# Feed-forward weights in units of four blocks: one load tile, one split and kept slots in a two-layer hybrid trunk

## The chip, the cores and the metric

The kernel runs on one core of one Trainium2 chip. The metric is device time in microseconds (us). TensorE (PE in the profile) does the matrix products, VectorE (DVE) and ScalarE (ACT) work on tiles in on-chip memory, GpSimd (POOL) does a few small things, and SyncE (SP) issues nearly all of the data transfers (DMA). Each engine takes its instructions strictly in the order in which they were put into its queue, and waits at an instruction until what it needs is there.

## The reference

The reference is a decoder trunk of two pre-norm residual layers on an input of 256 rows (positions) by 2048 columns, all in float32:

```python
def reference(...):
    h = x
    for layer in range(DEPTH):            # DEPTH = 2
        xn = rms_norm(h, norm_mix[layer])
        if layer % 2 == 0:
            mix = swa_mlstm_mixer(xn, w_in_even[j], w_out_even[j], ...)
        else:
            mix = forgetting_attention_mixer(xn, w_in_odd[j], fox_b_f[j], w_out_odd[j])
        h = h + mix
        h = h + swiglu(rms_norm(h, norm_ffn[layer]), w_gate[layer], w_up[layer], w_down[layer])
    return rms_norm(h, norm_final)

def swiglu(xn, w_gate, w_up, w_down):
    return (jax.nn.silu(xn @ w_gate) * (xn @ w_up)) @ w_down
```

The first layer's mixer is a sliding-window attention (16 heads) beside an mLSTM (4 heads), the second's is an attention with forget gates (16 heads). Each mixer has a wide input projection and an output projection of 2048 by 2048. The feed-forward part (FFN) has a hidden size of 5632, so three matrices of 2048 by 5632, and makes up most of the work.

## The kernel before

**Products.** A float32 product is made of three matmuls in a faster format. A matrix is split into `hi`, the value rounded to that format, and `lo`, the rest; the function `three` (line 508) adds hi·xh, lo·xh and hi·xl into one accumulator. The activations (`xh`, `xl`, `mh`, `ml`) are split once. The weights stream from memory: a block of 128 rows by 512 columns at a time is loaded raw, ScalarE copies it to `hi` (line 177 or 339), VectorE subtracts to get `lo` (line 178 or 340), and TensorE uses both. A plain load covers two blocks (`CK = 2`).

**Plain and mixed pairs.** `pair_group` (line 516) computes two column stripes of 512 at once, for the FFN a stripe of gate and one of up, or two stripes of down. It walks over pairs of row blocks in the order given by `ORDER` or `DOWN`. A plain pair takes eight `three` (24 matmuls). A mixed pair uses a scheme of the Strassen kind with seven (21 matmuls): it needs sums and differences of the weight blocks (`ta`, `tb`, `tc_`, `td`, lines 568 to 571, on VectorE), which are split as well, into the tiles `ht` and `lt`. It also needs sums of the activations (`sx`, `sd`), which are formed ahead. The mixed pairs collect four products `prods` in accumulators of their own over the whole group; at the group's end `combine` (line 523) works them into a tile `c` that is added to the plain accumulators.

**Stages.** A layer's FFN has 11 gate/up groups, in three parts (3, 4 and 4 groups). Each has 8 positions: 5 plain and 3 mixed pairs. After each gate/up group, `ffn` (line 599) adds (line 619), applies silu on ScalarE (line 621) and multiplies (line 623); then the result is turned, by DMA transposes on SP (line 648) or, for the last group of the first part, on TensorE. The turned values are joined and split into `mh`, `ml` some positions later. Each part ends with two down groups. `close_layer` (line 712) opens the pool `fp` for one layer's output projection (`out_proj`, line 493, through `gemm`) and its FFN.

**Buffers.** Before, pool `wp` gives six tiles each of `hi` and `lo`, two blocks a tile; pool `wr` four raw tiles of two blocks. In the FFN, the mixed pairs have four raw tiles of their own in `fp`, two tiles each of `ht` and `lt`, and a tile `t4` for two of the sums.

**Order.** The kernel is written as one loop nest; a planner at build time moves instructions among the engines' queues by its own costs and by which buffers are free, and what it gives is fixed: TensorE's queue mixes matmuls of several positions, and heads of the mixers with matmuls of a projection. How many buffers there are and when they come free therefore changes the order on every engine.

Of the kernel before, what the change touches and what calls it, by code (L numbers as in the profile page):

```python
# [17 lines left out]
P = 128  # L18
# [6 lines left out]
CK = 2  # L25
# [25 lines left out]
LATER_DOWN = (5, 6)  # L51
RAWS = 4
P_JOIN = 4
# [19 lines left out]
def trunk(  # L73
# [42 lines left out]

    def load_raw(w, k0, c0, n, pool=wr, bufs=4, raws=None):
        if raws:
            raw = raws.pop(0)
            raws.append(raw)  # L120
        else:
            raw = pool.tile([P, CK, NB], F32, tag="raw", name="raw", bufs=bufs)
        loaded[0] = nc.sync.dma_start(
            raw[:, :, 0:n], w[k0 * P : (k0 + CK) * P, c0 : c0 + n].rearrange("(k p) n -> p k n", p=P)
        )
        return raw
# [12 lines left out]
    load_x(0, CK)  # L139
    first = wr.tile([P, CK, NB], F32, tag="raw", name="raw", bufs=4)  # L140
    for k in range(CK):
# [31 lines left out]
    def split_chunk(raw, n):  # L173
        hi = wp.tile([P, CK, NB], F32R, tag="hi", name="hi")
        lo = wp.tile([P, CK, NB], F32R, tag="lo", name="lo")
        for k in (slice(0, 1), slice(1, CK)) if any(raw is f for f in fine) else (slice(0, CK),):
            latest[0] = nc.scalar.copy(hi[:, k, 0:n], raw[:, k, 0:n])  # L177
            nc.vector.tensor_tensor(  # L178
                out=lo[:, k, 0:n], in0=raw[:, k, 0:n], in1=hi[:, k, 0:n].bitcast(F32), op=ALU.subtract
            )  # L180
        return hi, lo

    def new_acc():
# [69 lines left out]
    def sums_of(pool, sh, sl, copies, full=None, tags=("tmp", "tmp"), bufs=None, box=None):  # L253
# [9 lines left out]
        nc.vector.tensor_tensor(out=s[:, 1, :], in0=s[:, 0, :], in1=full[:, 0, 0, :], op=ALU.subtract)  # L263
        nc.vector.tensor_tensor(out=s[:, 2, :], in0=full[:, 0, 0, :], in1=full[:, 0, 1, :], op=ALU.subtract)
        nc.vector.tensor_tensor(out=s[:, 3, :], in0=full[:, 1, 0, :], in1=s[:, 1, :], op=ALU.subtract)
# [61 lines left out]
    def scrap(fp, n):  # L327
        if n % 2 == 0:
            box = fp.tile([P, 4, NB], F32, tag="c", name="box", bufs=1)
            halves = box[:, 0:2, :], box[:, 2:4, :]  # L330
        elif n == 3:
            halves = [fp.tile([P, 3, NB], F32, tag=f"sd{i}", name="box", bufs=1)[:, 0:CK, :] for i in range(2)]
        else:
            halves = [fp.tile([P, CK, NB], F32, tag="raw", name="box", bufs=RAWS) for _ in range(2)]
        flat, turned = (a.rearrange("p a n -> p (a n)") for a in halves)
        return flat, turned.bitcast(U16).rearrange("p (b k t q) -> p b k t q", b=2, t=NT, q=P)
# [179 lines left out]
    def pair_group(fp, par, lhs, sums, mats, order, todo=(), halves=None, inner=None, raws=None):  # L516
# [6 lines left out]
        def combine(prods):  # L523
            c = fp.tile([P, 4, NB], F32, tag="c", name="c", bufs=1)
            nc.scalar.copy(c[:, 0, :], prods[0])
            nc.vector.tensor_tensor(out=c[:, 2, :], in0=prods[3], in1=c[:, 0, :], op=ALU.add)
            nc.vector.tensor_tensor(out=c[:, 1, :], in0=prods[2], in1=c[:, 2, :], op=ALU.add)
# [4 lines left out]
        for pos, (kind, pair) in enumerate(order):  # L532
            k0 = 2 * pair
            if inner is not None and pos == len(order) - 1:
                c = combine(prods)
                inner()
            if not kind:
                last = pos == len(order) - 1
                walk = [(i, t) for i in range(CK) for t in range(NT)]
                if last:  # L540
                    walk.sort(key=lambda it: it[1])
                for m, (w, c0) in enumerate(mats):
                    hi, lo = load_chunk(w, k0, c0, NB)
                    run_due(todo, pos)
                    for i, t in walk:
                        ah, al = lhs(k0 + i)
                        ts = slice(t * P, (t + 1) * P)
                        three(
                            plain[m][t], ah[:, ts], al[:, ts], hi[:, i, :], lo[:, i, :],
                            pos == 0 and i == 0, last and i == CK - 1,  # L550
# [3 lines left out]
            if first:  # L554
                prods = [bank(1 - par, "prod") for _ in range(4)]
            ra, rb = (load_raw(w, k0, c0, NB, fp, W_RAWS if halves else RAWS, raws) for w, c0 in mats)
            hg, lg = split_chunk(ra, NB)
            run_due(todo, pos)
            t4 = ra if halves else fp.tile([P, 2, NB], F32, tag="t4", name="t4", bufs=1)
            ta, tb, tc_, td = (  # L560
                (ra[:, 0, :], rb[:, 0, :], rb[:, 1, :], ra[:, 1, :])
                if halves
                else (t4[:, 0, :], t4[:, 1, :], ra[:, 0, :], ra[:, 1, :])
            )
            hu = wp.tile([P, CK, NB], F32R, tag="hi", name="hi")
            lu = wp.tile([P, CK, NB], F32R, tag="lo", name="lo")
            split_plain(hu[:, 1, :], lu[:, 1, :], rb[:, 1, :])
            nc.vector.tensor_tensor(out=ta, in0=rb[:, 0, :], in1=ra[:, 0, :], op=ALU.subtract)
            nc.vector.tensor_tensor(out=tb, in0=rb[:, 1, :], in1=rb[:, 0, :], op=ALU.subtract)
            nc.vector.tensor_tensor(out=tc_, in0=rb[:, 1, :], in1=ta, op=ALU.subtract)  # L570
            nc.vector.tensor_tensor(out=td, in0=ra[:, 1, :], in1=tc_, op=ALU.subtract)
            parts = []
            for src in (ra, rb) if halves else (t4, ra):
                if halves:
                    hs, ls = halves.pop(0)
                    halves.append((hs, ls))
                else:
                    hs = fp.tile([P, 2, NB], F32R, tag="ht", name="ht")
                    ls = fp.tile([P, 2, NB], F32R, tag="lt", name="lt")
                split_plain(hs, ls, src)  # L580
                parts.append((hs, ls))
            where = ((0, 0), (1, 0), (1, 1), (0, 1)) if halves else ((0, 0), (0, 1), (1, 0), (1, 1))
            ht = [parts[a][0][:, b, :] for a, b in where]
            lt = [parts[a][1][:, b, :] for a, b in where]
            sh, sl = sums(pair)
            xa, la = lhs(k0)
            xb, lb = lhs(k0 + 1)
            three(prods[0], xa[:, t0], la[:, t0], hg[:, 0, :], lg[:, 0, :], first, last)
            three(plain[0][0], xb[:, t0], lb[:, t0], hg[:, 1, :], lg[:, 1, :], False, False)
            three(plain[1][0], sh[:, 3, :], sl[:, 3, :], hu[:, 1, :], lu[:, 1, :], False, False)  # L590
            three(prods[1], sh[:, 0, :], sl[:, 0, :], ht[0], lt[0], first, last)
            three(prods[2], sh[:, 2, :], sl[:, 2, :], ht[1], lt[1], first, last)
            three(prods[3], sh[:, 1, :], sl[:, 1, :], ht[2], lt[2], first, last)
            three(plain[0][1], xb[:, t1], lb[:, t1], ht[3], lt[3], False, False)
        if inner is None:
# [3 lines left out]
    def ffn(layer, fp, sx, sd, key, todo, idx_next=None, key_next=None, finish=None):  # L599
# [6 lines left out]
        for g0, g1 in zip(PARTS, PARTS[1:]):  # L606
# [3 lines left out]
            for g in range(g0, g1):  # L610
# [5 lines left out]
                for m in range(2):  # L616
                    for t in range(NT):
                        o = c[:, 2 * m + t, :]
                        nc.vector.tensor_tensor(out=o, in0=plain[m][t], in1=o, op=ALU.add)
                for t in range(NT):  # L620
                    nc.scalar.activation(c[:, t, :], c[:, t, :], AF.Silu, scale=r[:, t : t + 1])
                for t in range(NT):
                    nc.vector.scalar_tensor_tensor(
                        out=c[:, t, :], in0=c[:, 2 + t, :], scalar=r[:, t : t + 1], in1=c[:, t, :], op0=ALU.mult, op1=ALU.mult
                    )
# [65 lines left out]
            for n0 in (0, 2):  # L691
# [13 lines left out]
                for m in range(2):  # L705
                    for t in range(NT):
                        o = h[:, t, (n0 + m) * NB : (n0 + m + 1) * NB]
                        nc.vector.tensor_tensor(out=o, in0=c[:, 2 * m + t, :], in1=o, op=ALU.add)
# [12 lines left out]

    acc0 = new_acc()
    hi = wp.tile([P, CK, NB], F32R, tag="hi", name="hi")
    lo = wp.tile([P, CK, NB], F32R, tag="lo", name="lo")
    latest[0] = latest_warm
# [596 lines left out]
```

## Time and profile before

| | |
|---|---|
| median of 3 runs | 2077.82 us |
| lowest and highest | 2076.74 and 2078.33 us |
| span of the profiled execution | 2076.6 us |
| granted TensorE clock, mean | 0.999 |
| TensorE busy | 2066.4 us |
| VectorE busy | 1824.5 us, 2410 instructions |
| ScalarE busy | 1374.7 us, 1736 instructions |
| DMA | 434.87 MB, 209 GB/s on the mean |

The times are those of whole executions. The profile is of one execution; its span, from its first to its last instruction, is 2076.6 us, and no separate time of that execution is given, so the span stands for it; the median of the runs is 1.2 us more. In a line of groups of instructions one reads the line of the kernel, the engine, the operation, output and inputs by the program's names with the tile's shape, the count, the busy time in us and the mean length in ns, then how long the engine had been idle before these and what ended it. In a line of the timeline the two first numbers are the start and the length in us; the length of an instruction reaches a little into the next, so the distance from start to start is what the engine's time is made of.

### The profile page before, as it was taken

Reading aid. Unit: us, or ns where it says so; the run is one execution under the profiler, and the core shown is the slowest. Engines: PE = TensorE matmul, PEld = TensorE weight load, DVE = VectorE, ACT = ScalarE, POOL = GpSimd, SP = SyncE. Lnnn points to the kernel's source line nnn. Section 1 sums busy time; section 2 is a strip of 40 time slices with the busy share of each in tenths; the row PEclk is TensorE's granted clock in tenths of the full one; section 3 lists DMA queues with packets and bytes.
Section 4 is the critical chain, followed back from the end, with each engine's and each line's share of the span. In section 5 each row is a group of like instructions: output and inputs, shape, how many; then the busy total and the mean of one; then the engine's idle time right before and its main releaser. Section 6 shows DMA issues by size and latency. Waiting matters only on the chain.

```text
span 2076.6 us, 26994 instructions
## 1 busy us (share of the span) xinstructions
PE 2066.4 (100%) x9473; PEld 1715.0 (83%) x9473; DVE 1824.5 (88%) x2410; ACT 1374.7 (66%) x1736; POOL 41.7 (2%) x66
## 2 busy tenths in 40 slices
PE   9999999999999999999999999999999999999998
PEld 7878888888888888888888888888888888888887
DVE  6788769999999999999899778689999999999994
ACT  6777678765676656667676776687655667456763
POOL 1010000000000000000000001000000000000000
PEclk9999999999999999999999999999999999999999
DMA  8566577666566666666576866586665667666764
GB/s 292 172 213 188 190 247 236 203 217 206 189 230 223 205 210 205 220 212 204 185 215 204 235 193 184 156 283 220 206 205 200 213 206 234 203 202 213 220 197 138
DMA packets 309575, 434.87 MB, mean 209 GB/s; under 512 B 106412, under 2 KB 114624, under 8 KB 309312
## 3 DMA queue, kind: packets, MB, share of 16 engines
q1 hardware_dynamic: 307088, 426.27, 65.1%
q0 software_dynamic: 1632, 5.80, 0.8%
q8 instruction: 74, 1.21, 0.2%
q10 hardware_dynamic: 720, 1.09, 0.2%
q14 instruction: 61, 0.50, 0.1%
HBM read 408.68 MB, written 2.12 MB: 198 GB/s over the span
## 4 chain that ended last, share of the span: by engine, by line
PE 97%; DVE 1%; ACT 1%; DMA 1%; issue 1%; SPq 0%; POOLq 0%; POOL 0%; ACTq 0%; DVEq 0%
PE acc L510 21%; PE acc L509 21%; PE acc L511 21%; PE acc L213 5%; PE acc L212 5%; PE acc L214 5%; PE prod L509 5%; PE prod L510 5%; PE prod L511 5%; PE p L369 1%; PE po L470 1%; DMA raw<-in_w_in_odd_dram 0%; ACT s L403 0%; PE po L471 0%; DVE lo L178 0%
## 5 line engine op out<-in xcount | busy, mean ns | idle before, releaser
L177 ACT CAST hi<-raw 128x1024 fp32r<-128x1024 f32 (+3 forms) x656 | 664.8, 1028 | 440.2 <-PE acc L511 269.1
L178 DVE TENSOR_TENSOR lo<-raw,hi 128x1024 fp32r<-128x1024 f32 (+3 forms) x656 | 772.8, 1192 | 146.3 <-ACT hi L177 143.5
L510 PE MATMUL acc<-lo,xh 128*128 128x512 f32 x1254 | 488.6, 390 | 0.0
L509 PE MATMUL acc<-hi,xh 128*128 128x512 f32 x1254 | 485.9, 390 | 0.5 <-ACT hi L177 0.5
L511 PE MATMUL acc<-hi,xl 128*128 128x512 f32 x1254 | 484.8, 389 | 0.0
L510 PEld LDWEIGHTS acc<-lo,xh 128*128 128x128 f32 x1254 | 235.4, 188 | 49.4 <-DVE lo L178 0.6
L509 PEld LDWEIGHTS acc<-hi,xh 128*128 128x128 f32 x1254 | 235.2, 188 | 49.5 <-ACT hi L177 0.7
L511 PEld LDWEIGHTS acc<-hi,xl 128*128 128x128 f32 x1254 | 235.4, 188 | 48.8
L510 PE MATMUL acc<-lo,mh 128*128 128x512 f32 x437 | 169.7, 389 | 0.0
L511 PE MATMUL acc<-hi,ml 128*128 128x512 f32 x437 | 168.4, 389 | 0.0
L509 PE MATMUL acc<-hi,mh 128*128 128x512 f32 x437 | 167.9, 389 | 0.0
L339 ACT CAST hi<-raw 128x512 fp32r<-128x512 f32 x109 | 67.6, 620 | 89.4 <-PE acc L511 80.5
L213 PE MATMUL acc<-lo,mh 128*128 128x512 f32 (+1 forms) x322 | 126.3, 392 | 0.0
L212 PE MATMUL acc<-hi,mh 128*128 128x512 f32 (+1 forms) x322 | 125.8, 391 | 0.0
L214 PE MATMUL acc<-hi,ml 128*128 128x512 f32 (+1 forms) x322 | 123.7, 391 | 0.0
L340 DVE TENSOR_TENSOR lt<-t,ht 128x1024 fp32r<-128x1024 f32 x95 | 115.8, 1219 | 5.2 <-ACT ht L339 5.1
L339 ACT CAST ht<-t 128x1024 fp32r<-128x1024 f32 x95 | 99.9, 1051 | 30.7 <-PE prod L511 28.8
L339 ACT CAST ht<-raw 128x1024 fp32r<-128x1024 f32 x95 | 99.7, 1050 | 29.7 <-PE acc L511 15.0
L340 DVE TENSOR_TENSOR lt<-raw,ht 128x1024 fp32r<-128x1024 f32 x95 | 115.7, 1218 | 1.8 <-ACT ht L339 1.8
L213 PE MATMUL acc<-lo,xh 128*128 128x512 f32 (+3 forms) x288 | 99.8, 348 | 0.2 <-DVE lo L178 0.2
L214 PE MATMUL acc<-hi,xl 128*128 128x512 f32 (+3 forms) x288 | 98.1, 344 | 0.0
L212 PE MATMUL acc<-hi,xh 128*128 128x512 f32 (+3 forms) x288 | 95.9, 347 | 0.3
(363 smaller groups left out, 3448.0 us busy)
## 6 DMA issues: line engine op xcount, KB each, us to landing
raw<-in_w_gate_dram SPq DMA_DIRECT2D x176, 512.0 KB, 4.5
raw<-in_w_up_dram SPq DMA_DIRECT2D x176, 512.0 KB, 4.6
raw<-in_w_down_dram SPq DMA_DIRECT2D x176, 512.0 KB, 5.1
raw<-in_w_in_odd_dram SPq DMA_DIRECT2D x88, 512.0 KB, 4.9
raw<-in_w_in_even_dram SPq DMA_DIRECT2D x51, 512.0 KB, 5.0
raw<-in_w_out_even_dram SPq DMA_DIRECT2D x32, 512.0 KB, 5.1
raw<-in_w_out_odd_dram SPq DMA_DIRECT2D x32, 512.0 KB, 4.8
hr<-in_w_in_even_dram SPq DMA_DIRECT2D x12, 512.0 KB, 4.6
```

Of the source, the lines that this page charges most:

```text
L177: latest[0] = nc.scalar.copy(hi[:, k, 0:n], raw[:, k, 0:n])
L178: nc.vector.tensor_tensor(out=lo[:, k, 0:n], in0=raw[:, k, 0:n], in1=hi[:, k, 0:n].bitcast(F32), op=ALU.subtract)
L212: nc.tensor.matmul(o, ah[:, ts], hi, start=(k == 0), stop=False)
L213: nc.tensor.matmul(o, ah[:, ts], lo, start=False, stop=False)
L214: nc.tensor.matmul(o, al[:, ts], hi, start=False, stop=(k == k_all - 1 and cs.stop == n))
L339: nc.scalar.copy(dst_h, src)
L340: nc.vector.tensor_tensor(out=dst_l, in0=src, in1=dst_h.bitcast(F32), op=ALU.subtract)
L369: nc.tensor.matmul(pq[j % 2][:, j // 2, :], q_of(j, b), k_of(j)[:, 0:cols], start=True, stop=True)
L470: nc.tensor.matmul(po, v_of(j, 0), tt[:, j, 0:2, :].rearrange("p c q -> p (c q)"), start=True, stop=False)
L509: nc.tensor.matmul(o, ah, hi, start=start, stop=False)
L510: nc.tensor.matmul(o, ah, lo, start=False, stop=False)
L511: nc.tensor.matmul(o, al, hi, start=False, stop=stop)
```

## The change

The change replaces the weight buffers by rings of slots of four blocks, and makes the FFN use a slot as a whole.

- `weights` is a list of three pairs `hi`, `lo` of four blocks; `raws_` a list of two raw tiles of four blocks. `slot` takes the next one round the ring, `half_slot` half of one, for all code that goes on with two blocks (the projections).
- For a layer's output projection and FFN, `close_layer` takes a fourth pair `hi3`, `lo3` from the pool `fp`, appends it to the ring, and removes it at the end.
- A plain pair in the FFN loads gate and up into one raw tile (two transfers), makes `hi` by two copies of two blocks and `lo` by one subtraction of four blocks.
- A mixed pair in the FFN loads into one raw tile of four blocks in `fp` (`RAWS`, now two of them) by three transfers: two blocks, then one, then one. One copy and one subtraction take the three blocks that are used as they are. The four sums are formed in place, two of them by one instruction whose first operand is repeated. Then two copies and one subtraction of four blocks split them into a second slot of the ring; `ht`, `lt` and `t4` are gone.
- `combine` in the FFN does the last two of its four additions in one instruction. The blocks of `c` stand in another order, two sums have the other sign, and in all mixed pairs the last four `three` stand in another order.

```diff
-RAWS = 4
+RAWS = 2
...
-    wp = ctx.enter_context(tc.tile_pool(name="wp", bufs=6))
-    wr = ctx.enter_context(tc.tile_pool(name="wr", bufs=4))
+    wp = ctx.enter_context(tc.tile_pool(name="wp", bufs=1))
+    weights = [[wp.tile([P, 4, NB], F32R, name=f"{a}{i}") for a in ("hi", "lo")] for i in range(3)]
+    wr = ctx.enter_context(tc.tile_pool(name="wr", bufs=1))
+    raws_ = [[wr.tile([P, 4, NB], F32, name=f"raw{i}")] for i in range(2)]
+    spare = {}
+
+    def slot(ring):
+        spare.pop(id(ring), None)
+        ring.append(ring.pop(0))
+        return ring[-1]
+
+    def half_slot(ring):
+        kept = spare.pop(id(ring), None)
+        if kept:
+            return [t_[:, CK:, :] for t_ in kept]
+        kept = slot(ring)
+        spare[id(ring)] = kept
+        return [t_[:, 0:CK, :] for t_ in kept]
...
     def split_chunk(raw, n):
-        hi = wp.tile([P, CK, NB], F32R, tag="hi", name="hi")
-        lo = wp.tile([P, CK, NB], F32R, tag="lo", name="lo")
+        hi, lo = half_slot(weights)
...
+    def load_rows(dst, w, k0, c0):
+        n = dst.shape[1]
+        loaded[0] = nc.sync.dma_start(
+            dst, w[k0 * P : (k0 + n) * P, c0 : c0 + NB].rearrange("(k p) n -> p k n", p=P)
+        )
+
+    def split_wide(hi, lo, src, parts):
+        for ks in parts:
+            latest[0] = nc.scalar.copy(hi[:, ks, :], src[:, ks, :])
+        nc.vector.tensor_tensor(out=lo, in0=src, in1=hi.bitcast(F32), op=ALU.subtract)
...
             nc.scalar.copy(c[:, 0, :], prods[0])
+            if halves is None:
+                nc.vector.tensor_tensor(out=c[:, 1, :], in0=prods[3], in1=c[:, 0, :], op=ALU.add)
+                nc.vector.tensor_tensor(out=c[:, 2, :], in0=prods[2], in1=c[:, 1, :], op=ALU.add)
+                nc.vector.tensor_tensor(
+                    out=c[:, 1:4:2, :],
+                    in0=prods[1].rearrange("p (a n) -> p a n", a=1).broadcast_to([P, 2, NB]),
+                    in1=c[:, 1:3, :],
+                    op=ALU.add,
+                )
+                return c
...
+                if halves is None:
+                    (raw,) = slot(raws_)
+                    for m, (w, c0) in enumerate(mats):
+                        load_rows(raw[:, CK * m : CK * (m + 1), :], w, k0, c0)
+                    hi, lo = slot(weights)
+                    split_wide(hi, lo, raw, (slice(0, CK), slice(CK, 4)))
+                    run_due(todo, pos)
...
+            if halves is None:
+                raw = fp.tile([P, 4, NB], F32, tag="raw", name="raw", bufs=RAWS)
+                (wa, ca), (wb, cb) = mats
+                load_rows(raw[:, 0:CK, :], wa, k0, ca)
+                for k in range(CK):
+                    load_rows(raw[:, 3 - k : 4 - k, :], wb, k0 + k, cb)
+                hi, lo = slot(weights)
+                split_wide(hi[:, 0:3, :], lo[:, 0:3, :], raw[:, 0:3, :], (slice(0, 3),))
+                run_due(todo, pos)
+                nc.vector.tensor_tensor(
+                    out=raw[:, 0:4:3, :],
+                    in0=raw[:, 3:4, :].broadcast_to([P, 2, NB]),
+                    in1=raw[:, 0:3:2, :],
+                    op=ALU.subtract,
+                )
+                nc.vector.tensor_tensor(out=raw[:, 2, :], in0=raw[:, 2, :], in1=raw[:, 0, :], op=ALU.subtract)
+                nc.vector.tensor_tensor(out=raw[:, 1, :], in0=raw[:, 1, :], in1=raw[:, 2, :], op=ALU.subtract)
+                ht_, lt_ = slot(weights)
+                split_wide(ht_, lt_, raw, (slice(0, CK), slice(CK, 4)))
...
     def close_layer(layer, w_out, idx, key, **rest):
         with tc.tile_pool(name=f"fp{layer}", bufs=2) as fp:
+            fourth = [fp.tile([P, 4, NB], F32R, name=f"{a}3", bufs=1) for a in ("hi", "lo")]
+            weights.append(fourth)
+            spare.clear()
             nx = len(mixed_of(ORDER))
...
             ffn(layer, fp, sx, sd, key, todo, **rest)
+            weights.remove(fourth)
+            spare.clear()
```

More of the change, by code (lines that the diff above doesn't have):

```diff
@@ L120, in load_raw @@
             raws.append(raw)
+        elif pool is None:
+            (raw,) = half_slot(raws_)
         else:
-            raw = pool.tile([P, CK, NB], F32, tag="raw", name="raw", bufs=bufs)
+            raw = pool.tile([P, CK, NB], F32, tag="raw", name="raw", bufs=W_RAWS)
         loaded[0] = nc.sync.dma_start(
@@ L139, in trunk @@
     load_x(0, CK)
-    first = wr.tile([P, CK, NB], F32, tag="raw", name="raw", bufs=4)
+    (first,) = half_slot(raws_)
     for k in range(CK):
@@ L333, in scrap @@
         else:
-            halves = [fp.tile([P, CK, NB], F32, tag="raw", name="box", bufs=RAWS) for _ in range(2)]
+            box = fp.tile([P, 4, NB], F32, tag="raw", name="box", bufs=RAWS)
+            halves = box[:, 0:CK, :], box[:, CK:, :]
         flat, turned = (a.rearrange("p a n -> p (a n)") for a in halves)
@@ L536, in pair_group @@
                 inner()
+            last = pos == len(order) - 1
             if not kind:
-                last = pos == len(order) - 1
                 walk = [(i, t) for i in range(CK) for t in range(NT)]
@@ L555, in pair_group @@
                 prods = [bank(1 - par, "prod") for _ in range(4)]
[L556 to L564, printed above, removed]
@@ L575, in pair_group @@
                     hs, ls = halves.pop(0)
                     halves.append((hs, ls))
[L577 to L583, printed above, removed]
@@ L584, in pair_group @@
-            lt = [parts[a][1][:, b, :] for a, b in where]
+                    split_plain(hs, ls, src)
+                    parts.append((hs, ls))
+                where = ((0, 0), (1, 0), (1, 1), (0, 1))
+                ht = [parts[a][0][:, b, :] for a, b in where]
+                lt = [parts[a][1][:, b, :] for a, b in where]
+                hg = [hg[:, 0, :], hg[:, 1, :], hu[:, 1, :]]
+                lg = [lg[:, 0, :], lg[:, 1, :], lu[:, 1, :]]
             sh, sl = sums(pair)
@@ L707, in ffn @@
                         o = h[:, t, (n0 + m) * NB : (n0 + m + 1) * NB]
-                        nc.vector.tensor_tensor(out=o, in0=c[:, 2 * m + t, :], in1=o, op=ALU.add)
+                        nc.vector.tensor_tensor(out=o, in0=c[:, 2 * t + m, :], in1=o, op=ALU.add)
                 for m in range(2):
```

63 lines of the change are left out of this document (38 added, 25 removed).

## The prediction

> **What bounds the kernel now.** I read the first part of the page, the throttle's row, the chain and TensorE's waits, in this order.
>
> ```profile
> span 2076.6 us, 26994 instructions
> PE 2066.4 (100%) x9473; PEld 1715.0 (83%) x9473; DVE 1824.5 (88%) x2410; ACT 1374.7 (66%) x1736; POOL 41.7 (2%) x66
> PEclk9999999999999999999999999999999999999999
> PE 97%; DVE 1%; ACT 1%; DMA 1%; issue 1%; SPq 0%; POOLq 0%; POOL 0%; ACTq 0%; DVEq 0%
> ```
> ```profile
> PE cold L159 <- POOL ones L156: 1.2, 1, 1.2
> PE acc L509 <- ACT hi L177: 0.5, 1, 0.5
> PE acc L213 <- DVE lo L178: 0.2, 1, 0.2
> ```
>
> TensorE is busy all the time at the full clock, makes 97% of the chain, and waited 1.9 us in all. So an instruction saved on another engine is worth nothing by itself, and the first matmul that has to wait costs its whole wait. The distance between matmuls follows from two rows with 20 matmuls between them: 21 steps in 4.76 us, 0.2267 us each.
>
> ```profile
> 1313.42 0.39 PE L212 MATMUL acc<-hi,mh 128*128 128x512 f32 x1
> ...
> 1318.18 0.39 PE L212 MATMUL acc<-hi,mh 128*128 128x512 f32 x1
> ```
>
> The engine to watch is VectorE. By stretch, in the feed-forward part (columns: stretch, length, then the busy time of PE, PEld, DVE, ACT, POOL, then clock and DMA):
>
> ```profile
> 576.00:617.00 41.00, 41.00 (x183) 33.94 (x182) 39.24 (x51) 28.04 (x31) 0.00 (x0) 1.00 0.63 205
> 596.30:613.80 17.50, 17.50 (x79) 14.48 (x78) 16.65 (x20) 11.89 (x13) 0.00 (x0) 1.00 0.60 172
> ```
>
> A gate/up group takes 5 plain positions of 24 matmuls and 3 mixed of 21, 183 x 0.2267 = 41.5 us. VectorE is busy 96% of the first stretch and TensorE waits for nothing: the buffers let VectorE be late here and early there. Whatever takes that freedom away decides this case.
>
> **The change, part by part.**
>
> *Fewer, longer instructions.* The built program has 1934 VectorE instructions against 2413, 1536 ScalarE against 1631, 95 more weight loads, and the same 9302 matmuls. Prices (columns: start, length):
>
> ```profile
> 663.78 4.62 DVE L178 TENSOR_TENSOR lo<-raw,hi 128x1024 fp32r<-128x1024 f32 x4
> 668.32 1.22 DVE L340 TENSOR_TENSOR lt<-t,ht 128x1024 fp32r<-128x1024 f32 x1
> 669.45 0.68 DVE L526 TENSOR_TENSOR c<-prod,c 128x512 f32<-128x512 f32 x1
> 670.17 0.69 DVE L527 TENSOR_TENSOR c<-prod,c 128x512 f32<-128x512 f32 x1
> ...
> 672.19 0.68 DVE L528 TENSOR_TENSOR c<-prod,c 128x512 f32<-128x512 f32 x1
> 672.79 0.68 DVE L529 TENSOR_TENSOR c<-prod,c 128x512 f32<-128x512 f32 x1
> ```
>
> Start to start, 1024 elements take (668.32 - 663.78)/4 = 1.13 us and 512 take 672.79 - 672.19 = 0.60; one that reads the result of the one just before it 670.17 - 669.45 = 0.72, so 0.12 more. On the line through these, 0.07 + 0.53 per 512, 1536 elements take 1.67 and 2048 take 2.20 us (my estimates; nothing of before is so long). The saving, 479 x 0.07 = 33 us, lies beside TensorE: nothing on the path.
>
> *The boundary between groups, the first loss.* The rows above show it in before: the shifted sums of the next group's first mixed pair (lt, 668.32) are split ahead of the combine (L526, 669.45), in buffers of their own. After the change these sums need a whole slot of four blocks in a ring of four, and that slot is held until the last products of the old group. In the built order, 77 matmuls = 17.48 us lie between the end of a group's last product and the first use of the next pair's split sums. VectorE has to do in them, in this order: combine 0.60 + 0.60, add 0.60, combine of two blocks 1.13, split 1536 for 1.67, three adds 1.80, sums 1.13, split 2048 for 2.20, two scalings 1.32, sum 0.60, split 1536 of the second mixed pair 1.67, sum 0.60, its sums 1.13 + 0.60 + 0.60, and last the split of 2048 that is waited for, 2.20. The scalings go by
>
> ```profile
> 559.08 1.41 DVE L623 SCALAR_TENSOR_TENSOR c<-c,r 128x512 f32<-128x512 f32 x2
> 560.40 0.69 DVE L340 TENSOR_TENSOR lo<-raw,hi 128x512 fp32r<-128x512 f32 x1
> ```
>
> (560.40 - 559.08)/2 = 0.66. The sum is 18.45; three direct dependences 0.36 and the ends (an instruction ends 0.09 after the next may start; start-up behind TensorE) some 0.1 more: 18.9, so 1.4 us late. Counted so for every boundary, 26 of them come out late, by 0.56 to 2.56, together 34 us. Nothing hides it: the list starts at a point of TensorE's own work, so a stall moves the next one along. Ends: without dependences and ends 0.9 x 26 = 23; with the two-block instructions, whose repeated operand no row shows, at the price of two single ones, and the slower dependent price for more of them, 1.8 x 26 = 47. I take 34, the value that the rows give.
>
> *The third mixed pair behind it.* With two raw tiles of four blocks, the third pair's three loads wait for the first pair's last split, and stand on SP's queue behind four transposes:
>
> ```profile
> 603.84 5.87 SPq L648 DMA_TRANSPOSE turned<-c  x4
> 609.82 0.53 SPq L123 DMA_DIRECT2D raw<-in_w_gate_dram  x1
> ```
> ```profile
> raw<-in_w_gate_dram SPq DMA_DIRECT2D x176, 512.0 KB, 4.5
> raw<-in_w_down_dram SPq DMA_DIRECT2D x176, 512.0 KB, 5.1
> ```
> ```profile
> L339 ACT CAST hi<-raw 128x512 fp32r<-128x512 f32 x109 | 67.6, 620 | 89.4 <-PE acc L511 80.5 <-ACT ht L339 4.3 <-issue 2.9
> L177 ACT CAST hi<-raw 128x1024 fp32r<-128x1024 f32 x620 | 643.0, 1051 | 423.5 <-PE acc L511 259.0 <-issue 48.5 <-PE acc L214 45.0
> ```
>
> From the group's last product: 13.3 us of the list above up to the second scaling, one copy 1.05, transposes 5.1 to 5.9 (another boundary's four took 5.1), landing 4.5 to 5.1, the copy of 1536 at 620 + 2 x 431 = 1.48: 25.5 to 27. Its first matmul stands 107 matmuls = 24.3 behind the same point, with the first stall 25.7: late by 0 to 1.3. Sixteen groups are followed so by another gate/up group: 5 to 22 us, and I take 0.8 x 16 = 13. In before the same loads follow the transposes at once, but onto four raw tiles, and no matmul waited.
>
> *The ends of the two mixers.* The fourth slot lies in the feed-forward pool, whose memory the mixers' pools still hold. Work of the output projection that filled TensorE while the last heads were finished now stands behind them. For the last heads of the second layer, before:
>
> ```profile
> 1301.68 1.91 PE L369 MATMUL p<-ktf,qtf 128*128 128x128 f32 x10
> ...
> 1318.41 0.27 PE L456 MATMUL pp<-ident,s 128*128 128x128 f32 x1
> ```
> ```profile
> 1304.57 1.28 DVE L372 SCALAR_TENSOR_TENSOR s<-p,cb 128x512 f32<-128x512 f32 x2
> 1305.88 1.22 DVE L388 TENSOR_REDUCE mx<-s 128x4 f32<-128x1024 f32 x1
> 1313.70 1.93 DVE L416 TENSOR_SCALAR s<-s,rec 128x128 f32<-128x128 f32 x8
> ```
> ```profile
> 1309.81 0.40 ACT L403 ACTIVATE s<-s,neg 128x128 f32<-128x128 f32 x1
> ...
> 1313.24 0.19 ACT L403 ACTIVATION_READ_ACCUMULATOR s<-s,neg 128x1 f32 x1
> ```
>
> Between scores and transposes TensorE had some 15 us of projection. In the new order it has three matmuls, 0.7, and the transposes themselves, 2.4. The softmax needs 0.7 + 1.2 + a split 1.1 + small ones 0.6 (half of it the gap from the last exponential to the scaling) + exponentials 3.6 (1309.81 to 1313.43) + scaling 1.9 = 9.1 to 9.4: stalled 6.3. Ends 5 (without the split) and 9 (the transposes not overlapped). For the mLSTM heads:
>
> ```profile
> 237.23 0.60 PE L1037 MATMUL pom<-ce,qst 128*128 128x257 f32 x2
> 237.67 0.59 PE L1035 MATMUL pom<-ve,dt__1241 128*128 128x257 f32 x2
> ```
> ```profile
> 253.36 0.91 ACT L344 ACTIVATE mh<-room,gT 128x256 fp32r<-128x256 f32 x2
> ```
>
> From a head's last product (L1037, done 237.7) to the first half of its split result, 253.8, lie 16 us, of which nearly 4 are other work that stood between on the two engines. In the new order 11 products at 237.67 - 237.23 = 0.44 and 5 matmuls, 5.9 us, are left there: stalled 6 to 10, I take 8. The upper end is 12, if the second head, which follows closer, adds its own.
>
> *A clock that cools* may add to this. No stretch of before shows it: the clock is 1.00 throughout. The Trainium skill, TensorE: Matmul & The Clock Gate, Part 1, says that an idle window of about 3.4 us halves the clock and that it takes as long to come back; by it, each of the two long stalls would cost 2 to 3.5 us more, an estimate, and the sum 5 us more. The boundary stalls are shorter than its window. I leave it out of the sum.
>
> *Nothing else:* the new order of threes and the signs change no count; 95 loads split in two cost SP 95 x some 0.4 (609.82 to the next issue, 0.5 at most), between issues that wait anyway; if that cover goes, it is in the 13 above.
>
> **Sum.** 34 + 13 + 6.3 + 8 = 61. On the profiled span 2076.6 that is 2138; the median of the runs lies 1.2 above that span: 2139. Ends: 23 + 5 + 5 + 6 = 39 gives 2117; 47 + 22 + 9 + 12 = 90 gives 2168.
>
> **Rivals.**
> *Faster.* VectorE gets through each boundary in time. For: 33 us less of fixed cost. Against: the list is a sum of measured rates, and it is the per-element part that fills the window. It decides from 1.4 us less per boundary, so from 1.5 instead of 2.20 us for a 2048 split. The waits to be won are 1.9 us and the few matmuls that start late, and the mixers' ends must be hidden too: 2072. The Trainium skill, VectorE: DVE Perf Modes, section on the TRN2 errata, says that a large tile pays the fixed cost once and many small ones each time; by that advice alone this would be the case. It speaks of one engine's time, not of when a slot comes free.
> *No change.* The stalls are there only in my count, since leads taken earlier cover them: 2078. Against it: the boundary's list starts at a matmul, no earlier lead enters.
> *Only the mixers' ends stall.* The boundaries are covered, 6.3 + 8: 2092.
> *More.* The late loads push later loads, so each boundary loses 3 us or more where I have 2, and the clock cools: 2077.8 + 26 x 3 + 14 + 5 = 2175.
>
> **How the numbers follow.** 0.2% (4.2 us) is what a measurement tells from no change. My sum within its ends 0.65, only the mixers 0.10, more 0.14, no change 0.05, faster 0.06. Leaving out the upper case's tail and the two lowest cases, the range is 2092 to 2170. Slower 0.89, same 0.05, faster 0.06.
>
> **What would show it.** Waits of the boundary matmuls (TensorE's products prod and acc in the function of the three matmuls) for the long split, L210, some 1 to 2.6 us each; waits of matmuls for a copy, L209, behind late loads; two gaps of 6 to 10 us, ahead of the transposes of the second layer's last heads and of the first layer's projection rows 8 to 11. A split of 2048 that takes 2.3 us confirms the price. If those waits are missing and VectorE idles ahead of the combine, the step on the boundary is wrong.

## The result, and the profile after

The changed kernel takes 2196.23 us (median of 4 runs, 2192.77 to 2201.11) against 2078.07 us before on the same chips: a ratio of 1.0572, 95% interval 1.0555 to 1.0588. The prediction had the direction, slower, and put the size at 61 us; it is 118 us, and 2196 lies above the range. The profiled execution's span grew by 114.5 us.

The first lines of the page of the changed kernel, and its chain:

```profile
span 2191.1 us, 26291 instructions
PE 2103.9 (96%) x9473; PEld 1715.9 (78%) x9473; DVE 1798.8 (82%) x1931; ACT 1353.5 (62%) x1641; POOL 40.7 (2%) x66
PE 38%; DVE 22%; DMA 8%; issue 8%; ACT 7%; SPq 2%; DVEq 0%; ACTq 0%; POOLq 0%; POOL 0%
```

VectorE executes 479 instructions fewer, and is busy 25.7 us less, as the edit says. TensorE is no longer the whole chain: VectorE has 22% of it. TensorE's waits (engine and tile, line, what it waited for: total, times, longest):

```profile
PE prod L540 <- DVE lo L210: 24.8, 22, 1.2
PE prod L539 <- ACT hi L209: 21.0, 31, 2.0
PE pp L486 <- DVE s L446: 7.2, 1, 7.2
PE acc L241 <- ACT mh L374: 7.2, 1, 7.2
PE acc L540 <- DVE lo L210: 5.2, 5, 1.6
PE acc L539 <- DVE h L383: 3.0, 6, 1.1
PE prod L539 <- ACT c L555: 2.7, 2, 1.7
```

Before, all waits were 1.9 us. By TensorE's own landmarks (the first and last matmul of each feed-forward part, from the timelines) the time went to four places:

| stretch | before | after | more |
|---|---|---|---|
| end of the mLSTM and first output projection | 95.4 | 108.0 | 12.6 |
| first feed-forward part and second layer's input projection | 959.4 | 1006.4 | 47.0 |
| last attention heads and second output projection | 98.5 | 111.2 | 12.8 |
| second feed-forward part, up to its last pair group | 644.0 | 686.7 | 42.7 |

The remaining stretches differ by half a microsecond together. One boundary between two gate/up groups, VectorE's timeline of the changed kernel (start, length, idle time ahead in brackets):

```profile
618.10 0.69 DVE L557 TENSOR_TENSOR c<-prod,c 128x512 f32<-128x512 f32 x1 [1.03 <-PE prod L541]
618.89 0.69 DVE L558 TENSOR_TENSOR c<-prod,c 128x512 f32<-128x512 f32 x1
619.50 0.68 DVE L684 TENSOR_TENSOR c<-acc,c 128x512 f32<-128x512 f32 x1
620.10 1.22 DVE L559 TENSOR_TENSOR c<-prod,c 128x1024 f32<-128x1024 f32 x1
621.23 1.75 DVE L210 TENSOR_TENSOR lo<-raw,hi 128x1536 fp32r<-128x1536 f32 x1
622.90 1.88 DVE L684 TENSOR_TENSOR c<-acc,c 128x512 f32<-128x512 f32 x3
624.69 2.28 DVE L210 TENSOR_TENSOR lo<-raw,hi 128x2048 fp32r<-128x2048 f32 x1
626.89 1.22 DVE L615 TENSOR_TENSOR raw<-raw 128x1024 f32<-128x1024 f32 x1
...
631.63 1.22 DVE L615 TENSOR_TENSOR raw<-raw 128x1024 f32<-128x1024 f32 x1
632.76 0.68 DVE L622 TENSOR_TENSOR raw<-raw 128x512 f32<-128x512 f32 x1
633.36 0.68 DVE L621 TENSOR_TENSOR raw<-raw 128x512 f32<-128x512 f32 x1
634.08 0.69 DVE L622 TENSOR_TENSOR raw<-raw 128x512 f32<-128x512 f32 x1
635.00 4.49 DVE L210 TENSOR_TENSOR lo<-raw,hi 128x2048 fp32r<-128x2048 f32 x2 [0.23 <-ACT hi L209]
```

These are the instructions of the prediction's list at its prices; a few neighbours have changed places (the split at 624.69 stands ahead of the sums at 626.89, for one). The list starts when the product that the combine reads first is done, and runs 19.2 us (618.10 to the end of the first of the last two splits, 635.00 + 2.29) with 0.23 us of idle time in it. TensorE's side of the same boundary:

```profile
634.15 0.39 PE L541 MATMUL acc<-hi,sx 128*128 128x512 f32 x1
635.02 0.50 PE L539 MATMUL prod<-hi,sx 128*128 128x512 f32 x1 [0.49 <-ACT hi L209]
635.36 0.39 PE L539 MATMUL acc<-hi,xh 128*128 128x512 f32 x1
635.59 0.63 PE L539 MATMUL prod<-hi,sx 128*128 128x512 f32 x2
637.35 0.55 PE L540 MATMUL prod<-lo,sx 128*128 128x512 f32 x1 [1.13 <-DVE lo L210]
637.70 0.63 PE L541 MATMUL prod<-hi,sx 128*128 128x512 f32 x1
638.13 0.63 PE L540 MATMUL acc<-lo,xh 128*128 128x512 f32 x1
```

There are two waits. The first is for a copy to hi, the second for the split. Each shows in the steps between starts: 0.87 for 0.23 at the first, 1.53 for 0.23 (from the last of the two at 635.59) at the second, so 1.95 us together. The copy follows the first pair's last sum (L622 at 632.76), but not at once. ScalarE's timeline:

```profile
631.08 1.05 ACT L209 CAST hi<-raw 128x1024 fp32r<-128x1024 f32 x1 [3.13 <-DVE raw L621]
632.03 1.99 ACT L716 COPY c<-c 128x1024 uint16<-128x1024 uint16 x2
633.93 2.94 ACT L209 CAST hi<-raw 128x1024 fp32r<-128x1024 f32 x3
```

The sum was done at 633.44. The copy started 0.49 us later, behind the two copies (L716) that prepare the old group's result for the transposes. All 16 first waits of this kind in the trace stand so: the copy follows L716 without idle time, 0.49 us after the end of its sum. VectorE's 0.23 us of idle time ahead of the split is a wait for the same copy.

After each of TensorE's waits, the next step takes 0.34 or 0.35. From 637.70 on, the steps are 0.43: the clock has fallen to half, as the windows of the two stretches of 3.4 us show (columns as before: busy times, then clock and DMA):

```profile
637.70:641.10 3.40, 3.40 (x9) 2.65 (x8) 1.80 (x1) 1.22 (x2) 0.00 (x0) 0.50 0.94 72
641.10:644.50 3.40, 3.40 (x16) 2.80 (x15) 2.29 (x1) 0.90 (x2) 0.00 (x0) 1.00 1.05 373
```

The sum over all feed-forward matmuls of the step less 0.227 us, sorted by what released each, gives for both layers: waits for the long split (L210) 34.9 us; waits for a copy (L209) directly ahead of these 13.0; other waits for copies 16.6; the slow first steps after waits 11.7 (3.0 or less of that before); steps at half clock 6.0; others, such as the residual L383 and the combine's own copy L555, some 9.

The two long gaps:

```profile
253.10 0.80 PE L241 MATMUL acc<-hi,mh 128*128 128x512 f32 x1 [7.17 <-ACT mh L374]
```
```profile
1373.59 1.45 PE L486 MATMUL pp<-ident,s 128*128 128x128 f32 x4 [7.22 <-DVE s L446]
```

After the first the clock stays at one half from 253.10 to 258.8, another 2.8 us lost; after the second until 1378.4, 2.4 us.

### The profile page after: what moved, and what is told of

Its sections match the earlier page's. It is cut to its first block, busy times and chain, and to the rows that moved or that the text cites. A ratio compares the mean times of both kernels' runs of the same rounds, so it can differ in the third digit from the quotient of the medians.

```text
span 2191.1 us, 26291 instructions
## 1 busy us (share of the span) xinstructions
PE 2103.9 (96%) x9473; PEld 1715.9 (78%) x9473; DVE 1798.8 (82%) x1931; ACT 1353.5 (62%) x1641; POOL 40.7 (2%) x66
## 4 chain that ended last, share of the span: by engine, by line
PE 38%; DVE 22%; DMA 8%; issue 8%; ACT 7%; SPq 2%; DVEq 0%; ACTq 0%; POOLq 0%; POOL 0%
PE acc L540 9%; PE acc L541 9%; DVE lo L210 8%; PE acc L539 8%; ACT hi L209 4%; DMA raw<-in_w_up_dram 3%; DMA raw<-in_w_down_dram 3%; DVE raw L615 3%; PE prod L540 2%; PE prod L541 2%; PE prod L539 2%; DVE raw L621 2%; DVE c L684 2%; PE acc L241 1%; PE acc L243 1%
## 5 line engine op out<-in xcount | busy, mean ns | idle before, releaser
L209 ACT CAST hi<-raw 128x1024 fp32r<-128x1024 f32 (+1 forms) x607 | 653.2, 1116 | 506.7 <-PE acc L541 169.6
L210 DVE TENSOR_TENSOR lo<-raw,hi 128x2048 fp32r<-128x2048 f32 (+1 forms) x351 | 745.9, 2143 | 140.2 <-ACT hi L209 139.0
L540 PE MATMUL acc<-lo,xh 128*128 128x512 f32 x1320 | 515.7, 391 | 0.0
L541 PE MATMUL acc<-hi,xl 128*128 128x512 f32 x1320 | 514.3, 390 | 0.0
L196 DVE TENSOR_TENSOR lo<-raw,hi 128x1024 fp32r<-128x1024 f32 (+3 forms) x239 | 270.0, 1145 | 120.7 <-ACT hi L195 119.9
L195 ACT CAST hi<-raw 128x1024 fp32r<-128x1024 f32 (+3 forms) x239 | 230.9, 985 | 140.9 <-PE acc L243 25.8
L615 DVE TENSOR_TENSOR raw<-raw 128x1024 f32<-128x1024 f32 x95 | 116.0, 1221 | 1.0
L540 PEld LDWEIGHTS acc<-lo,mh 128*128 128x128 f32 x466 | 87.8, 189 | 25.4 <-DVE lo L210 7.3
L539 PEld LDWEIGHTS acc<-hi,mh 128*128 128x128 f32 x466 | 87.4, 188 | 21.0 <-ACT mh L369 2.6
L541 PEld LDWEIGHTS acc<-hi,ml 128*128 128x128 f32 x466 | 87.7, 188 | 19.2 <-DVE ml L370 0.7
```

The costliest lines, as they stand in the source:

```text
L196: nc.vector.tensor_tensor(out=lo[:, k, 0:n], in0=raw[:, k, 0:n], in1=hi[:, k, 0:n].bitcast(F32), op=ALU.subtract)
L209: latest[0] = nc.scalar.copy(hi[:, ks, :], src[:, ks, :])
L210: nc.vector.tensor_tensor(out=lo, in0=src, in1=hi.bitcast(F32), op=ALU.subtract)
L539: nc.tensor.matmul(o, ah, hi, start=start, stop=False)
L540: nc.tensor.matmul(o, ah, lo, start=False, stop=False)
L541: nc.tensor.matmul(o, al, hi, start=False, stop=stop)
```

## The experiments

The question was what makes the boundaries late. The prediction's cause was the slot: the sums of the next pair have to wait for a whole slot of a shared ring. Its rival is the length: the far end of a subtraction of 2048 elements, of which nothing is released until all is done. All times stand beside runs of the kernel before on the same chip, 2077.4 to 2077.7 us.

**The fourth slot after the output projection.** (Two runs.)

```diff
-            weights.append(fourth)
-            spare.clear()
...
             todo = out_proj(w_out, idx, key, (*sx, fp))
+            weights.append(fourth)
+            spare.clear()
```

> The fourth slot joins the ring only after the output projection, which then has six half slots as before. Theory 'mixers' (the late memory of the fourth slot pushes the projection's matmuls behind the mixers' last heads): the two stretches that grew from 95.4 to 108.0 us and from 98.4 to 111.3 go back to about 96 and 99, the cold clock behind the two long gaps goes too; time 2196 - 25 = 2171. Rival (other heads' work was late for another reason, for instance ScalarE): both gaps of 7 us stay, 2196.

Measured: 2186.79 us. Both long gaps are gone; the stretches are 95.3 and 100.2 us, 23.8 us less than in the changed kernel. So it is the fourth slot in the ring during the projection that put the projection's work behind the heads. That the reason is its memory, which the mixers still hold, fits the code and was not tried apart. The time is 9.4 us less and not the 25 expected, for the feed-forward stretches grew by 10.0 and 9.3 us. The ring stands at another slot when the feed-forward part begins, and the planner gave another order; 33 matmuls wait there for the long split in place of 27 (waits as in the rows above, L210), and the steps at half clock make 11.2 in place of 6.0 us. That the ring's position decides this was not tried apart. Part of the growth is the clock of this one execution: its mean was 0.993 at 2189.01 us, and 0.998 at 2184.57 us in the other.

**Subtractions of 1024 in place of 2048.** (Two runs.) Slots, loads, sums and combine stay.

```diff
         for ks in parts:
             latest[0] = nc.scalar.copy(hi[:, ks, :], src[:, ks, :])
-        nc.vector.tensor_tensor(out=lo, in0=src, in1=hi.bitcast(F32), op=ALU.subtract)
+            nc.vector.tensor_tensor(out=lo[:, ks, :], in0=src[:, ks, :], in1=hi[:, ks, :].bitcast(F32), op=ALU.subtract)
```

> Each copy of two blocks in the feed-forward part is followed by its own subtraction of 1024 elements, as before; slots, loads, sums and the combine stay as in the changed kernel. Theory 'slot' (the boundary list is late because the slot of four blocks comes free late): slots come free as late as they did, VectorE has 256 more fixed costs of 0.07 us; feed-forward waits as they were, time 2196, plus or minus 10. Theory 'width' (what is late is the far end of a 2048 subtraction, of which nothing can be used before all is done, and what stands behind it on VectorE): the waits for the split at 1.3 us and most of the waits for copies vanish, 2196 less 60 to 90 = 2106 to 2136, with the two gaps at the mixers still there.

Measured: 2110.51 us, 86 less than the changed kernel, with the slots untouched. TensorE's waits of this run, down to the two that were at the top:

```profile
PE acc L241 <- ACT mh L374: 7.2, 1, 7.2
PE pp L486 <- DVE s L446: 7.0, 1, 7.0
...
PE prod L539 <- ACT hi L209: 0.6, 2, 0.4
PE prod L540 <- DVE lo L210: 0.5, 3, 0.2
```

The waits for splits and copies are as good as gone, also those of the third mixed pair, although its loads still stand behind four transposes. So the shared ring alone does not make TensorE wait. It may still be needed for the loss: the sums' split stands behind the combine here too, where the kernel before has a split of sums ahead of it. A run with subtractions of 2048 and as many buffers for the sums as before was not made.

**Both edits.** (Four runs.)

> The two edits together: fourth slot after the output projection, subtractions of 1024. Theory 'width': both losses gone, 2080 to 2105. Theory 'slot': only the mixers' 25 us are won, 2171, plus or minus 10.

Measured: 2090.41 us, ratio to before 1.0060 (1.0044 to 1.0077). The place of the fourth slot and the length of the subtraction account for 106 of the 118 us. VectorE's boundary now (the same group, timeline of this run):

```profile
590.31 0.69 DVE L557 TENSOR_TENSOR c<-prod,c 128x512 f32<-128x512 f32 x1 [0.28 <-PE prod L541]
...
606.32 2.35 DVE L210 TENSOR_TENSOR lo<-raw,hi 128x1024 fp32r<-128x1024 f32 x2
608.59 0.68 DVE L621 TENSOR_TENSOR raw<-raw 128x512 f32<-128x512 f32 x1
609.30 0.69 DVE L622 TENSOR_TENSOR raw<-raw 128x512 f32<-128x512 f32 x1
610.43 4.88 DVE L210 TENSOR_TENSOR lo<-raw,hi 128x1024 fp32r<-128x1024 f32 x4 [0.44 <-ACT hi L209]
```
```profile
610.66 0.39 PE L540 MATMUL prod<-lo,sx 128*128 128x512 f32 x1
```

The first pair's split sums are the two halves at 606.32; the four at 610.43 are the second pair's and a plain pair's. The halves are done 17.2 and 18.4 us after 590.31, and TensorE wants the first of them at 610.66, after 20.35. Two things moved. On VectorE the first half is there 2 us earlier than the whole split of the changed kernel (19.2 us): a half takes 1.1 us less than the whole, and the split now stands ahead of the second pair's last two sums (608.59, 609.30), where it stood behind them. And the built order leaves more room: for this group 91 matmuls, 20.7 us, between the product that starts the list and the first use of the next pair's split sums, where the changed kernel had 77, 17.5 us. These 3.2 us alone are more than the 1.95 us by which the changed kernel was late. So the length acts through the planner's order as well as by itself, and the runs do not part the two.

**The sums in a slot of their own, subtractions wide.** (Two runs.) The ring keeps three slots, the fourth is used for ht and lt alone.

```diff
-            weights.append(fourth)
-            spare.clear()
+            own[0] = fourth
...
-                ht_, lt_ = slot(weights)
+                ht_, lt_ = own[0]
```

> The split sums of the mixed pairs have the fourth slot for themselves and the ring keeps three; the wide subtractions stay. Also no fourth slot during the output projection, so the mixers' 25 us should be won in any case. Theory 'slot' (sharing a ring with the weights is what makes the sums late): feed-forward loss of 90 us mostly gone, 2080 to 2110. Theory 'width': the boundary stays late by 1 to 2 us, 2150 to 2185.

Measured: 2260.85 us, slower than the changed kernel by 65. TensorE's two largest waits (helper lines are one further down here):

```profile
PE prod L541 <- DVE lo L211: 52.3, 44, 1.6
PE prod L540 <- ACT hi L210: 46.8, 53, 4.0
```

Both theories missed: the slot theory wanted it faster, and the length theory gave at most 2185. With one slot for the sums every pair, not only the first of a group, waits until the pair ahead is used up: 44 waits for the split in place of 22.

**The same, subtractions of 1024.** (Two runs.)

> All subtractions of 1024; the mixed sums have the fourth slot for themselves, the ring keeps three. Theory 'width' alone (how slots are shared does not matter once the pieces are short): as with the shared ring, 2085 to 2095. Theory 'slot after all' (a single slot for the sums makes the second mixed pair wait for the first, and the wide split made it worse in the run before): slower than the shared ring by 10 us or more, 2100 to 2130.

Measured: 2102.99 us, as the second theory of the expectation has it. With short pieces the own slot costs 13 us over the shared ring, with long ones 74 (2260.85 less 2186.79). So the number of slots matters, and the length decides how much. The shared ring is better than one slot of the sums' own. The kernel before had two tiles of two blocks each way for them, so this is no test of its arrangement.

**Which subtraction.** Fourth slot late; only the sums' subtraction in halves, then only the plain pairs'. (Two runs each.)

```diff
-    def split_wide(hi, lo, src, parts):
+    def split_wide(hi, lo, src, parts, by_part=False):
...
-                split_wide(ht_, lt_, raw, (slice(0, CK), slice(CK, 4)))
+                split_wide(ht_, lt_, raw, (slice(0, CK), slice(CK, 4)), True)
```

> Fourth slot after the output projection; of the wide subtractions only those of the mixed pairs' sums are made as two of 1024 (each right behind its copy); plain pairs keep one of 2048. Theory 'waited-for split' (late is the one subtraction of 2048 that the first products of the next group wait for): nearly as good as both halved, 2088 to 2105. Theory 'coarse queue' (any long subtraction holds up what stands behind it on VectorE, so plain ones count as much, 161 of 256): about 40% of the way from 2187 to 2090, 2140 to 2160.

> The mirror image: fourth slot after the output projection; plain pairs' subtractions as two of 1024, the mixed sums' as one of 2048. Theory 'waited-for split': little won over 2187, 2160 to 2190. Theory 'coarse queue': about 60% of the way to 2090, 2120 to 2140.

Measured: 2116.82 us with the sums in halves, 2161.21 with the plain pairs in halves; 2186.79 with neither and 2090.41 with both. The parts add up: 70.0 + 25.6 = 95.6 of 96.4, with the runs of one of these kernels up to 5.5 us apart. The 95 subtractions of the sums carry nearly three quarters, the 161 of the plain pairs one quarter. The first number lies between the two theories, the second at the lower end of what 'waited-for split' gave. The plain ones do not only stand in the queue: with the sums in halves, TensorE waited nine times, 6.8 us in all, for one of the plain pairs' long subtractions.

**The sum of the list.** (Two runs.) The changed kernel without the two products of gate and up after each group; as its expectation says, the feed-forward part is then wrong.

> The changed kernel without the two instructions after each gate/up group that multiply the gate by the up values (the feed-forward part is computed wrongly; nothing else is left out). VectorE has 1.3 us less to do between a group's last product and the split that the next group waits for; slots, loads and lengths stay. Theory 'list' (the sum of VectorE's work in that window is what is late): each of some 20 boundaries 1.3 us better, and what follows on them, 2196 - 26 - 10 to 20 = 2150 to 2160. Rival (loads, copies on ScalarE or the slots' release set the boundary): 2185 to 2196.

Measured: 2144.59 us, 51.6 less for 1.3 us less on VectorE in each of 22 groups, 29 us. TensorE's wait for the long split:

```profile
PE prod L540 <- DVE lo L210: 14.1, 22, 1.3
```

In the changed kernel this row has 24.8, and the waits of prod for a copy are 4.8 here in place of 21.0 us. The time lies even below the 2150 to 2160 of theory 'list', far from the rival's. So the work that the boundary's list holds is what TensorE waits for, and each microsecond of it is paid about 1.8 times; that the rest is slow first steps, the clock and what follows on a late split was not measured apart. Nor does the run part VectorE from ScalarE: the copies L716 no longer wait for the products, and no wait for a copy of the sums follows on them any more.

**What is left.** Two edits to the version with both: the combine's last two additions as two instructions again, and the split of three blocks as 1024 and 512. (Four runs each.)

```diff
-                nc.vector.tensor_tensor(
-                    out=c[:, 1:4:2, :],
-                    in0=prods[1].rearrange("p (a n) -> p a n", a=1).broadcast_to([P, 2, NB]),
-                    in1=c[:, 1:3, :],
-                    op=ALU.add,
-                )
+                nc.vector.tensor_tensor(out=c[:, 3, :], in0=prods[1], in1=c[:, 2, :], op=ALU.add)
+                nc.vector.tensor_tensor(out=c[:, 1, :], in0=prods[1], in1=c[:, 1, :], op=ALU.add)
```

> As the version with both edits (2090.4), and the combine's last two additions are again two of 512 in place of one of two blocks. Theory 'the remaining 13 us come from the join and the order of the feed-forward part': same as with one, 2085 to 2095. Rival (the combine's long instruction, which needs both earlier sums, holds up the boundary as the long split did): 2078 to 2084.

```diff
-                split_wide(hi[:, 0:3, :], lo[:, 0:3, :], raw[:, 0:3, :], (slice(0, 3),))
+                split_wide(hi[:, 0:3, :], lo[:, 0:3, :], raw[:, 0:3, :], (slice(0, CK), slice(CK, 3)))
```

> As the version with both edits (2090.4), and the split of three blocks (one copy and one subtraction of 1536) made as 1024 and 512, each subtraction right behind its copy. Theory 'length' (all that is left is the last long instruction): most of the 13 us go, 2078 to 2084. Rival (what is left are waits for the joined values and the start of each part, which no split sets): 2087 to 2093.

Measured: 2093.08 us (ratio to before 1.0078, 1.0061 to 1.0095) and 2092.72 us (1.0072, 1.0054 to 1.0090). Neither takes the remaining 13 us away, so these two long instructions are not its cause. In the version with both edits, the lag behind before grows in single steps (by equal counts of matmuls: 2.3 us from the end of the first part nearly to the end of the last gate/up group, 6.1 at the end of the first layer's feed-forward part, 8.7 in the second layer's, 12 at its last pair groups), and its waits are many small ones:

```profile
PE acc L539 <- ACT mh L369: 2.2, 2, 1.6
PE cold L178 <- POOL ones L175: 1.2, 1, 1.2
PE acc L539 <- ACT hi L195: 1.0, 1, 1.0
PE prod L539 <- ACT c L555: 0.8, 2, 0.4
```

What sets these was not settled. No version was found that beats the kernel before, which has under 2 us of waits to give.

## Why the prediction was wrong, point by point

- *What bounds the kernel.* Right: TensorE without waits, nothing to win from saved instructions. 479 instructions less made nothing faster.
- *The boundary, 34 us.* The mechanism, VectorE's sum between a group's last product and the next pair's split sums, was right: the list came nearly in that order, took 19.2 us for 18.9, and taking 1.3 us out of it gave 51.6 us. The price of a 2048 subtraction too: 2.28 us long, 2.21 from start to start. The number of late boundaries, 26, was near too: the rows have 27 waits for the long split. The term was mis-sized: the waits for the split and for the copy just ahead of it are 47.9 us (34.9 and 13.0). At the boundary shown they make TensorE 1.95 us late, where the prediction had 1.4. Two parts of the difference are seen. I let VectorE begin when the last product's step ends, 0.23 us after its start, but the rows show such a matmul with 0.39. And ScalarE is not in the list: the split stood idle 0.23 us for a copy that stood behind two copies of L716.
- *Its cause, the slot.* Not enough. That the sums "need a whole slot of four blocks in a ring of four" does not by itself make them late: with halves and the ring as it is the waits are gone (2110.51), and with a slot of their own they grow (2260.85). In its place the runs show the length of the subtractions, three quarters of it those of the sums, and the order that the planner builds from it. Whether long subtractions with more buffers would do as well stays open.
- *The third mixed pair, 13 us.* Its 13.3 us up to the second scaling hold a split of 1536 and a sum that the list names only behind the scalings; the trace has them in the order of the 13.3 us. The other waits for copies are 16.6 us, and that this is near is luck. At the boundary shown the loads behind the transposes made no matmul wait. In the gate/up groups a matmul waited for the copy of a mixed pair's own blocks (prod from hi and xh) at four places, 4.8 us in all, and not at sixteen; the other waits stand elsewhere. Nor are they a loss of their own: with short subtractions they go although the transposes are still ahead on SP's queue. How they hang on the late split was not followed.
- *The ends of the mixers, 14.3 us.* The waits are 7.2 and 7.2 us, 14.4 in all, against 8 and 6.3; that the sum fits to 0.1 us is two errors that cancel. The stretches grew by 25.4: the half clock behind each gap and smaller waits behind it are the rest.
- *The clock, left out.* This was the wrong choice. The rule of the Trainium skill (TensorE: Matmul & The Clock Gate, Part 1), that an idle window of about 3.4 us halves the clock, agrees with the two long gaps: half clock from 253.10 to 258.8 and up to 1378.4. The fall came 2.6 and 5.2 us into the gaps. I took from it that stalls shorter than the window leave the clock alone, and there the trace differs: the 3.4 us ahead of 637.70 held 0.65 + 1.30 us of waiting, and the clock fell. It did so at four places of the feed-forward part, and at others with the same waits it did not; what parts them is told at the end.
- *What a wait costs besides itself.* Not in the sum at all, and put at nothing without a reason: the first step after each wait takes 0.34 in place of 0.23 us, 11.7 us in the feed-forward parts.
- *The sum.* 34 + 13 + 14.3 against 47.9 + 16.6 + 14.4 in waits, and some 35 us that stand behind waits: slow first steps, half clock, later waits for residual and joined values. This is the step that failed most: the prediction added up waits and let nothing follow on them. The rival named More, with longer stalls from late loads and a clock that cools, put the time at 2175, still too low.

## What to carry to other kernels

When one engine feeds another with little slack, the unit of an instruction is also the unit of its release: four blocks in one subtraction save some 0.07 us of fixed time, and hold the first block back by 1.1 us. Merge what nobody waits for, and keep short what the bound engine wants next and what stands ahead of it. When waits are added up, count what each one brings along: here a microsecond of lateness was paid almost twice.

And look from when on a new buffer can be used: here a fourth slot joined the ring while the mixers were still at work, the projection's work fell in behind them, and what had filled TensorE meanwhile was gone.

## What was not expected of the hardware

The clock fell to half after waits of 0.65 and 1.30 us inside 3.4 us (637.70 to 641.10 at 0.50), so short waits that follow each other closely can do it. When they do shows in the times at which the granted clock changed: in this execution all of them lie whole multiples of 3.413 us apart (falls at 248.54, 637.66, 743.47, 1371.53, 1753.82 and 2020.06). The pair of waits 0.65 and 1.30 stands at eleven boundaries. At three of them (637.35, 1753.41, 2019.68) both waits lie inside one stretch of this grid, and exactly there the clock fell at the stretch's end. At the other eight an edge of the grid parts the pair (682.03 at the next one, in the middle of the second wait), and it did not. The fourth fall, at 743.47, follows a wait of 1.87 us and the start of another in one stretch. So which boundaries lose the clock depends on where the grid lies. Whether this is why the four executions, with mean clocks of 0.990 to 0.995, differ by 8 us was not followed.

The first matmul after a wait is followed by a slow step: 0.31 to 0.35 in place of 0.227 us at the 71 waits of more than 0.15 us at full clock in the feed-forward functions. An addition with a repeated operand over two blocks (L559) took 1217 ns, as much as any addition of 1024 elements:

```profile
L559 DVE TENSOR_TENSOR c<-prod,c 128x1024 f32<-128x1024 f32 x33 | 40.2, 1217 | 0.2
```
